# Down projection of a decoder trunk on one core: seven and eight pairs of K-blocks as seven products, instead of six and six

## The chip, the cores and the metric

The kernel runs on one core of a Trainium2 chip. The core has a matmul engine (TensorE; its weight loads are shown as a row of their own, PEld), VectorE (DVE), ScalarE (ACT), GpSimd (POOL) and SyncE (SP), whose queue issues nearly all loads. The metric is the device time of one execution in microseconds (us), less is better.

## The reference, cut to what matters

One layer of a decoder: a token mixer, and then the feed-forward part that this document is about. With 256 tokens, a model width of 2048 and a hidden width of 5632, all in float32:

```python
    h = rms_norm(x, pre_ffn_g[l])
    f = (jax.nn.silu(h @ w_gate[l]) * (h @ w_up[l])) @ w_down[l]
    x = x + rms_norm(f, post_ffn_g[l])
```

The product with `w_down` (5632 x 2048) is the down projection.

## The kernel before, in words

**Splitting.** Every float32 operand is split into a high part (`hi`, a cast on ScalarE) and a low part (`lo`, the difference, on VectorE). A product of two blocks is three matmuls into one PSUM bank: high by high, low by high and high by low (`product`, lines 664 to 666). Weights come from memory in pieces of 512 KB (128 partitions x 1024 numbers, two K-blocks by 512 columns) into four load buffers (`raw`), and their parts go into pools of five buffers each (`hi`, `lo`).

**Halves.** The down projection (`down_columns`) makes 1024 of the 2048 output columns in one call, as two chunks of 512, and is called twice: the first and the second half. In each the 44 K-blocks of 128 are taken as 22 pairs. A pair has 2 K-blocks, 2 token blocks of 128 and 2 chunks of columns, which is 8 products of blocks.

**Plain and seven-product pairs.** A plain pair (`plain_pair`, "P") does the 8 products, 24 matmuls. The other kind (`seven_products`, "S") gets the same 8 from 7 products of sums, as Strassen's scheme does, 21 matmuls. For that it needs sums of the hidden activations (`token_sums`, once for all columns) and sums of the weights (lines 629 and 635, on VectorE, in each half anew). The sums are split again: `hi_sb`/`lo_sb` and `hi_sa`/`lo_sa`. A P has two low parts to make, an S has a low part of 1024 columns, one of 512 (`lo_22`), four sums of 512 columns and two more low parts. TensorE takes the products of an S in the order of the tiles `hi`, `hi_22`, `hi_sb`, `hi_sa`; its 12th matmul is the first that reads `lo_sb`.

**Order.** A text of 20 letters gives the order of P and S pairs in a half; two plain pairs (20 and 21) close it, ordered by bank, so that the banks are done one after the other and can be closed: the partial sums of the S products are added (`partial_sums`, after the last S), squares are summed for the norm and gains multiplied (`close_chunk`, `close_last`), and at the very end the scaled output is stored (`scale_out`). In both halves the text is PPSPPSPPSPPSPPSPPSPP, with S for pairs 4 to 9. I count the steps of a half from 0. The engines run their queues in order; a framework places the instructions of each queue, somewhat ahead of the program's order.

Of the kernel before, what the change touches and what calls it, by code (L numbers as in the profile page):

```python
# [8 lines left out]
F32 = mybir.dt.float32  # L9
F32R = mybir.dt.float32r  # L10
AF = mybir.ActivationFunctionType
# [3 lines left out]
P = 128  # L15
# [18 lines left out]
def trunk(  # L34
# [23 lines left out]
    nc = tc.nc  # L58
# [70 lines left out]
    def load_in_order(dst, src):  # L129
        tc.keep_in_program_order(nc.sync.dma_start(out=dst, in_=src))  # L130
# [424 lines left out]
    hpool = ctx.enter_context(tc.tile_pool(name="hpool", bufs=1, side="right"))  # L555
# [4 lines left out]
    def h_chunk(c):  # L560

        if c not in h_parts:
            n = 2 if c < 8 else 1
            part = hpool.tile([P, 2, 4 * n, T], F32R, tag=f"h{c}", name=f"h{c}")
            for j in range(n):
                h_parts[c + j] = (part, 4 * j)
        part, k0 = h_parts[c]
        return part[:, 0, k0:k0 + 4], part[:, 1, k0:k0 + 4]
# [6 lines left out]
    sums = {}  # L575
# [189 lines left out]
    dn = ctx.enter_context(tc.tile_pool(name="dn", bufs=1))  # L765
    ss_f = const.tile([P, NT, 4], F32, tag="ss_f", name="ss_f")
# [3 lines left out]
    def hidden_sums(c):  # L770
        hi, lo = h_chunk(c)
        tmp = dn.tile([P, 2, 1024], F32, tag="wide", name="sums_f")
        home = dn.tile([P, 2, 2, 4, P], F32R, tag=f"sums{c}", name=f"sums{c}")
        token_sums(c, 2, hi, lo, tmp, home)

    def down_columns(n0, new_fg, seq, extra, finish, tail_pairs, order):

        gp = [ft.tile([P, 512], F32, tag="fa", name="gp") for _ in range(2)]
        for j in range(2):
            load_in_order(gp[j], post_ffn[(n0 + j) * 512:(n0 + j + 1) * 512].partition_broadcast(P))  # L780
        kinds = [k for k, _ in seq]
        last_s = max(i for i, k in enumerate(kinds) if k == "S")
        banks, product = products_into(kinds + ["P"] * len(tail_pairs), bank_in(dict(enumerate(
            ("tr", "acc", "acc", "acc", "tr", "mx", "mx", "acc")))))
        srcs = (w_down[n0], w_down[n0 + 1])
        for i, (k, p) in enumerate(seq):
            if i in extra:
                extra[i]()
            if k == "P":
                parts = plain_pair(srcs, p, h_of)  # L790
            else:
                h22 = dn.tile([P, 512], F32R, tag="h22", name="hi_22")
                l22 = dn.tile([P, 512], F32R, tag="l22", name="lo_22")
                parts = seven_products(srcs, p, h_of, sums[p // 2, p % 2], h22, l22)
            for part in parts:
                for b, a, w in part:
                    product(b, a, w)
            advance()
            if i == last_s:
                fg = new_fg()  # L800
                partial_sums(banks, fg[:, 0, 0:512], fg[:, 0, 512:1024], fg[:, 1, 0:512], fg[:, 1, 512:1024])
        parts = [plain_pair(srcs, p, h_of) for p in tail_pairs]
        where = {1: (0, 0), 2: (0, 1), 3: (1, 0), 7: (1, 1)}

        def run(*bs):
            for j in range(2):
                for prods in parts:
                    for b, a, w in prods[j]:
                        if b in bs:
                            product(b, a, w)  # L810

        for bs in order:
            run(*bs)
            for b in bs:
                finish(n0, *where[b], fg, banks[b], gp)

    def close_chunk(n0, tb, j, fg, bank, gp):
        cs = slice(j * 512, (j + 1) * 512)
        n = n0 + j
        nc.vector.tensor_tensor(out=fg[:, tb, cs], in0=fg[:, tb, cs], in1=bank, op=ALU.add)  # L820
        sq = dn.tile([P, 512], F32, tag="u", name="sq_f")
        nc.scalar.activation(out=sq, in_=fg[:, tb, cs], func=AF.Square, accum_out=ss_f[:, tb, n:n + 1])
        nc.vector.tensor_tensor(out=fg[:, tb, cs], in0=fg[:, tb, cs], in1=gp[j], op=ALU.mult)

    def sequence(pattern, s_pairs, p_pairs):
        s_it, p_it = iter(s_pairs), iter(p_pairs)
        return [(k, next(s_it if k == "S" else p_it)) for k in pattern]
# [3 lines left out]
    def new_fg(pool, tag):  # L831
        fgs.append(pool.tile([P, NT, 1024], F32, tag=tag, name=f"fg{len(fgs)}"))
        return fgs[-1]

    pattern = "PPSPPSPPSPPSPPSPPSPP"
    down_columns(0, lambda: new_fg(dn, "wide"), sequence(pattern, range(4, 10), [0, 1, 2, 3] + list(range(10, 20))),
                 {0: lambda: hidden_sums(2), 5: lambda: hidden_sums(3), 11: lambda: hidden_sums(4)}, close_chunk, [20, 21],
                 [(1, 3), (2, 7)])

    def scale_out(tb, chunks):  # L840
        for c in chunks:
# [6 lines left out]
    def close_last(n0, tb, j, fg, bank, gp):  # L848
        cs = slice(j * 512, (j + 1) * 512)
        n = n0 + j  # L850
        nc.vector.tensor_tensor(out=fg[:, tb, cs], in0=fg[:, tb, cs], in1=bank, op=ALU.add)
        sq = dn.tile([P, 512], F32, tag="u", name="sq_f")
        nc.scalar.activation(out=sq, in_=fg[:, tb, cs], func=AF.Square, accum_out=ss_f[:, tb, n:n + 1])
        if (tb, j) == (1, 0):
            scale_out(0, (1, 2))
        if j == 0:
            nc.vector.tensor_tensor(out=fg[:, tb, cs], in0=fg[:, tb, cs], in1=gp[j], op=ALU.mult)
            nc.vector.tensor_reduce(out=part_ss[:, tb:tb + 1], in_=ss_f[:, tb, 0:3], axis=AX.X, op=ALU.add)
            nc.vector.tensor_scalar(out=part_ss[:, tb:tb + 1], in0=part_ss[:, tb:tb + 1], scalar1=1.0 / D, scalar2=EPS,
                                    op0=ALU.mult, op1=ALU.add)  # L860
            return
        nc.vector.scalar_tensor_tensor(out=ss_t[:, tb:tb + 1], in0=ss_f[:, tb, 3:4], scalar=1.0 / D,
                                       in1=part_ss[:, tb:tb + 1], op0=ALU.mult, op1=ALU.add)
        nc.gpsimd.tensor_tensor(out=ro_f[:, tb:tb + 1], in0=ss_t[:, tb:tb + 1], in1=neg_half[:, :1], op=ALU.pow)
        nc.vector.tensor_tensor(out=fg[:, tb, cs], in0=fg[:, tb, cs], in1=gp[j], op=ALU.mult)
        if tb == 0:
            scale_out(0, (0,))
        else:
            scale_out(1, (0, 1, 2))
            scale_out(0, (3,))  # L870
            scale_out(1, (3,))

    down_columns(2, lambda: new_fg(hpool, "h0"), sequence(pattern, range(4, 10), [0, 1, 2, 3] + list(range(10, 20))),
                 {}, close_last, [20, 21], [(1,), (2,), (3,), (7,)])


def _layout(inputs):
# [86 lines left out]
```

## Time and profile before

| | us |
|---|---|
| median of 3 runs (1127.82 to 1128.39) | 1127.92 |
| the profiled execution's own time | 1127.93 |
| its span, first to last instruction | 1126.2 |
| TensorE busy in the span | 1113.6 |
| VectorE busy | 817.0 |
| ScalarE busy | 578.4 |

The profile is of one execution. Times of rows are us from the start of the span. The rest of the execution's own time, 1.7 us, lies around the span. An engine that is busy for a part of the span can still set the time of the stage in which others wait for it.

### The profile page before, as it was taken

To read this page: it belongs to the slowest core of one execution; us is meant where nothing else is said; L and a number is where in the kernel's file an instruction comes from. 1 tells how busy PE (TensorE), PEld (TensorE's weight loads), DVE (VectorE), ACT (ScalarE), POOL (GpSimd) and SP (SyncE) were. 2 spreads that over 40 slices of the span, in tenths; PEclk is the share of its full clock that TensorE was granted. 3 is DMA by queue.
4 is the path that set the end of the run, shared out by engine and by line. 5 is a ranking of instruction groups with operands and counts; after the bars stand their busy time and mean duration, and the time that the engine had idled before them with its cause. 6 is when DMAs were issued, how large, how long until landed. Compare 5 with 4: busy or idle time off the path is not lost.

```text
span 1126.2 us, 14203 instructions
## 1 busy us (share of the span) xinstructions
PE 1113.6 (99%) x5198; PEld 937.4 (83%) x5198; DVE 817.0 (73%) x1039; ACT 578.4 (51%) x792; POOL 27.5 (2%) x55
## 2 busy tenths in 40 slices
PE   9999999999999999999999999999999999999996
PEld 7888899998888878888888888888888888888885
DVE  6655555656778488797888987888655787777775
ACT  7644445655644356455455545445444454554451
POOL 0000000000200001000000000000000000000000
PEclk9999999999999999999999999999999999999998
DMA  9855555566566547467457457556655456665662
GB/s 355 267 190 185 169 161 182 162 217 194 170 195 235 186 148 227 154 195 235 164 183 239 157 187 233 178 187 221 204 192 187 145 191 225 220 214 194 213 213 86
DMA packets 65014, 221.35 MB, mean 197 GB/s; under 512 B 7344, under 2 KB 9392, under 8 KB 64432
## 3 DMA queue, kind: packets, MB, share of 16 engines
q1 hardware_dynamic: 64656, 220.30, 59.8%
q8 instruction: 40, 0.66, 0.2%
q14 instruction: 30, 0.25, 0.1%
q10 hardware_dynamic: 288, 0.15, 0.1%
HBM read 218.32 MB, written 2.10 MB: 196 GB/s over the span
## 4 chain that ended last, share of the span: by engine, by line
PE 96%; DVE 2%; DMA 1%; issue 1%; ACT 0%; POOL 0%; POOLq 0%; DVEq 0%; ACTq 0%; SPq 0%
PE bank L666 16%; PE bank L664 16%; PE bank L665 16%; PE acc L88 15%; PE acc L90 14%; PE acc L89 14%; PE h_ps L687 1%; DMA raw<-in_w_down_dram 1%; PE qk_ps L235 0%; PE sc L267 0%; DMA cols<-in_cols_dram 0%; PE yt_ps L191 0%; DVE x_lo L499 0%; DVE lo L81 0%; PE o_ps L243 0%
## 5 line engine op out<-in xcount | busy, mean ns | idle before, releaser
L81 DVE TENSOR_TENSOR lo<-raw,hi 128x1024 fp32r<-128x1024 f32 (+2 forms) x353 | 415.8, 1184 | 233.8 <-ACT hi L79 224.2
L79 ACT CAST hi<-raw 128x1024 fp32r<-128x1024 f32 (+2 forms) x353 | 358.0, 1018 | 341.4 <-PE acc L89 148.4
L88 PE MATMUL acc<-hi,x_hi 128*128 128x512 f32 (+1 forms) x640 | 244.5, 382 | 0.7 <-ACT x_hi L183 0.7
L89 PE MATMUL acc<-hi,x_lo 128*128 128x512 f32 (+1 forms) x640 | 239.5, 374 | 0.0
L90 PE MATMUL acc<-lo,x_hi 128*128 128x512 f32 (+1 forms) x640 | 239.2, 375 | 0.0
L664 PE MATMUL bank<-hi,x_hi 128*128 128x512 f32 x416 | 162.5, 391 | 0.0
L666 PE MATMUL bank<-lo,x_hi 128*128 128x512 f32 x416 | 161.9, 389 | 0.0
L665 PE MATMUL bank<-hi,x_lo 128*128 128x512 f32 x416 | 161.8, 389 | 0.0
L88 PEld LDWEIGHTS acc<-hi,x_hi 128*128 128x128 f32 x640 | 120.6, 188 | 19.5 <-issue 2.0
L90 PEld LDWEIGHTS acc<-lo,x_hi 128*128 128x128 f32 x640 | 120.5, 188 | 18.3
L89 PEld LDWEIGHTS acc<-hi,x_lo 128*128 128x128 f32 x640 | 120.7, 189 | 17.0 <-DVE x_lo L184 0.2
L664 PE MATMUL bank<-hi,h 128*128 128x512 f32 x280 | 109.1, 390 | 0.0
L665 PE MATMUL bank<-hi,h 128*128 128x512 f32 x280 | 108.9, 389 | 0.0
L666 PE MATMUL bank<-lo,h 128*128 128x512 f32 x280 | 108.9, 389 | 0.0
L666 PEld LDWEIGHTS bank<-lo,x_hi 128*128 128x128 f32 x416 | 78.1, 188 | 16.3
L665 PEld LDWEIGHTS bank<-hi,x_lo 128*128 128x128 f32 x416 | 78.1, 188 | 16.0
L664 PEld LDWEIGHTS bank<-hi,x_hi 128*128 128x128 f32 x416 | 78.1, 188 | 15.9
L634 ACT CAST hi_sb<-raw 128x1024 fp32r<-128x1024 f32 x28 | 29.4, 1051 | 112.7 <-DVE raw L629 103.3
L664 PEld LDWEIGHTS bank<-hi,h 128*128 128x128 f32 x280 | 52.6, 188 | 11.1 <-DVE h L691 0.4
L666 PEld LDWEIGHTS bank<-lo,h 128*128 128x128 f32 x280 | 52.6, 188 | 10.9
L665 PEld LDWEIGHTS bank<-hi,h 128*128 128x128 f32 x280 | 52.6, 188 | 10.9
L629 DVE TENSOR_TENSOR raw<-raw 128x512 f32<-128x512 f32 x84 | 58.0, 690 | 1.9
(214 smaller groups left out, 1210.0 us busy)
## 6 DMA issues: line engine op xcount, KB each, us to landing
raw<-in_w_gate_dram SPq DMA_DIRECT2D x88, 512.0 KB, 4.3
raw<-in_w_up_dram SPq DMA_DIRECT2D x88, 512.0 KB, 4.5
raw<-in_w_down_dram SPq DMA_DIRECT2D x88, 512.0 KB, 4.4
raw<-in_w_ret_dram SPq DMA_DIRECT2D x47, 512.0 KB, 4.2
raw<-in_w_diff_dram SPq DMA_DIRECT2D x48, 384.0 KB, 3.2
raw<-in_w_out_dram SPq DMA_DIRECT2D x32, 512.0 KB, 3.6
raw<-in_w_sgu_dram SPq DMA_DIRECT2D x16, 512.0 KB, 3.9
x_sb<-in_x_dram SPq DMA_DIRECT2D x2, 1024.0 KB, 8.3
```

Source lines behind the costliest of these rows:

```text
L79: nc.scalar.copy(out=hi, in_=raw)
L81: nc.vector.tensor_tensor(out=lo, in0=raw, in1=hi.bitcast(F32), op=ALU.subtract)
L88: nc.tensor.matmul(ps, lhsT=a_hi, rhs=wh, start=first, stop=False)
L89: nc.tensor.matmul(ps, lhsT=a_lo, rhs=wh, start=False, stop=False)
L90: nc.tensor.matmul(ps, lhsT=a_hi, rhs=wl, start=False, stop=last)
L629: nc.vector.tensor_tensor(out=out, in0=in0, in1=in1, op=op)
L634: nc.scalar.copy(out=h3, in_=rb)
L664: nc.tensor.matmul(banks[b], lhsT=a_hi, rhs=w_hi, start=start, stop=False)
L665: nc.tensor.matmul(banks[b], lhsT=a_lo, rhs=w_hi, start=False, stop=False)
L666: nc.tensor.matmul(banks[b], lhsT=a_hi, rhs=w_lo, start=False, stop=left[b] == 0)
L687: nc.tensor.transpose(out=pt[:, i], in_=aa[tb][:, i * P:(i + 1) * P], identity=ident)
```

## The change

The second letter text is replaced by two: the first half gets a seventh S (pair 10), the second half a seventh and an eighth (pairs 10 and 11). Pairs 10 and 11 need token sums of their own (`sums_10`, `sums_11`), made one pair at a time. Their tiles take space that is free by then; for that the hidden chunks 0 and 1, which shared a tile, get one each. The squares of the closing steps, whose values nobody reads (only their sum), are written into the PSUM bank that was just read instead of a buffer of their own.

```diff
-            n = 2 if c < 8 else 1
+            n = 2 if 2 <= c < 8 else 1
...
+    def hidden_sums_of_pair(c, q, tmp, home):
+        hi, lo = h_chunk(c)
+        token_sums((c, q), 1, hi[:, 2 * q:2 * q + 2], lo[:, 2 * q:2 * q + 2], tmp, home)
+        sums[c, q] = sums[(c, q), 0]
+
+    def sums_10():
+        hidden_sums_of_pair(5, 0, dn.tile([P, 2, 512], F32, tag="wide", name="sums_f"),
+                            dn.tile([P, 2, 1, 4, P], F32R, tag="sums5", name="sums5"))
+
+    def sums_11():
+        hidden_sums_of_pair(5, 1, hpool.tile([P, 2, 512], F32, tag="h0", name="sums_f"),
+                            hpool.tile([P, 2, 1, 4, P], F32R, tag="h1", name="sums11"))
...
-        sq = dn.tile([P, 512], F32, tag="u", name="sq_f")
-        nc.scalar.activation(out=sq, in_=fg[:, tb, cs], func=AF.Square, accum_out=ss_f[:, tb, n:n + 1])
+        nc.scalar.activation(out=bank, in_=fg[:, tb, cs], func=AF.Square, accum_out=ss_f[:, tb, n:n + 1])
...
-    pattern = "PPSPPSPPSPPSPPSPPSPP"
-    down_columns(0, lambda: new_fg(dn, "wide"), sequence(pattern, range(4, 10), [0, 1, 2, 3] + list(range(10, 20))),
-                 {0: lambda: hidden_sums(2), 5: lambda: hidden_sums(3), 11: lambda: hidden_sums(4)}, close_chunk, [20, 21],
-                 [(1, 3), (2, 7)])
+    down_columns(0, lambda: new_fg(dn, "wide"),
+                 sequence("PPSPPSPPSPPSPSPSPSPP", range(4, 11), [0, 1, 2, 3] + list(range(11, 20))),
+                 {0: lambda: hidden_sums(2), 5: lambda: hidden_sums(3), 9: lambda: hidden_sums(4), 13: sums_10},
+                 close_chunk, [20, 21], [(1, 3), (2, 7)])
...
-    down_columns(2, lambda: new_fg(hpool, "h0"), sequence(pattern, range(4, 10), [0, 1, 2, 3] + list(range(10, 20))),
-                 {}, close_last, [20, 21], [(1,), (2,), (3,), (7,)])
+    down_columns(2, lambda: new_fg(hpool, "h0"),
+                 sequence("PPSPPSPSPSPPSPSPSPSP", range(4, 12), [0, 1, 2, 3] + list(range(12, 20))),
+                 {9: sums_11}, close_last, [20, 21], [(1,), (2,), (3,), (7,)])
```

How the queues change, at three places. First SyncE's queue in the second part of the first half (lines with - stood there before, lines with + stand there now). L77 loads the pieces of plain pairs, L601 those of S pairs; "x4" are four equal ones in a row.

```order
 L77 DMA raw<-in_w_down_dram 128x1024 x4
 L601 DMA raw<-in_w_down_dram 128x1024 x2
-L77 DMA raw<-in_w_down_dram 128x1024 x4
-L601 DMA raw<-in_w_down_dram 128x1024 x2
-L77 DMA raw<-in_w_down_dram 128x1024 x4
+L77 DMA raw<-in_w_down_dram 128x1024 x2
+L601 DMA raw<-in_w_down_dram 128x1024 x2
+L77 DMA raw<-in_w_down_dram 128x1024 x2
+L601 DMA raw<-in_w_down_dram 128x1024 x2
+L77 DMA raw<-in_w_down_dram 128x1024 x2
 L601 DMA raw<-in_w_down_dram 128x1024 x2
 L77 DMA raw<-in_w_down_dram 128x1024 x12
```

From step 11 on two loads of a plain pair, and no longer four, stand between those of two S pairs.

Second, VectorE's queue at step 8 of the first half, an S pair (`lo`, `lo_22`, here with its number, the sums of weights, `lo_sb`, `lo_sa`), as it was before:

```order
L605 TENSOR_TENSOR lo<-raw,hi 128x1024
L605 TENSOR_TENSOR lo_7893<-raw,hi_7892 128x512
L629 TENSOR_TENSOR raw<-raw 128x512 x3
L635 TENSOR_TENSOR raw<-raw 128x512
L605 TENSOR_TENSOR lo_sb<-raw,hi_sb 128x1024
L605 TENSOR_TENSOR lo_sa<-raw,hi_sa 128x1024
```

and as it is now, from `lo_22` on, with the token sums of pair 10 (`sums_f`) between:

```order
L605 TENSOR_TENSOR lo_7894<-raw,hi_7893 128x512
L629 TENSOR_TENSOR raw<-raw 128x512
L582 TENSOR_TENSOR sums_f<-h_5606 128x512
L629 TENSOR_TENSOR raw<-raw 128x512
L586 SCALAR_TENSOR_TENSOR sums_f<-sums_f 128x128
L629 TENSOR_TENSOR raw<-raw 128x512
L587 SCALAR_TENSOR_TENSOR sums_f<-sums_f 128x128
L635 TENSOR_TENSOR raw<-raw 128x512
L589 TENSOR_TENSOR sums_f<-sums_f 128x128
L590 TENSOR_TENSOR sums_f<-sums_f 128x128
L605 TENSOR_TENSOR lo_sb<-raw,hi_sb 128x1024
L605 TENSOR_TENSOR lo_sa<-raw,hi_sa 128x1024
```

Five operations have come into this S pair, ahead of `lo_sb`. (The sums of chunk 4, too, stand where they stood, at step 5.)

Third, the end of the second half on VectorE, from the last S on: low parts of plain pairs (L81), the adding of partial sums (L673 to L676) and the first closing operation (L851 before, L863 now). Before:

```order
L605 TENSOR_TENSOR lo_sa<-raw,hi_sa 128x1024
L81 TENSOR_TENSOR lo<-raw,hi 128x1024 x3
L673 TENSOR_TENSOR fg_9177<-fg_9177,bank_8581 128x512
L674 TENSOR_TENSOR fg_9177<-fg_9177,bank_8585 128x512
L81 TENSOR_TENSOR lo<-raw,hi 128x1024
L675 TENSOR_TENSOR fg_9177<-fg_9177,bank_8577 128x512
L676 TENSOR_TENSOR fg_9177<-fg_9177,bank_8577 128x512
L81 TENSOR_TENSOR lo<-raw,hi 128x1024 x4
L851 TENSOR_TENSOR fg_9177<-fg_9177,bank_8479 128x512
```

and now:

```order
L605 TENSOR_TENSOR lo_sa<-raw,hi_sa 128x1024
L81 TENSOR_TENSOR lo<-raw,hi 128x1024 x3
L673 TENSOR_TENSOR fg_9255<-fg_9255,bank_8596 128x512
L81 TENSOR_TENSOR lo<-raw,hi 128x1024
L674 TENSOR_TENSOR fg_9255<-fg_9255,bank_8600 128x512
L81 TENSOR_TENSOR lo<-raw,hi 128x1024
L675 TENSOR_TENSOR fg_9255<-fg_9255,bank_8592 128x512
L676 TENSOR_TENSOR fg_9255<-fg_9255,bank_8592 128x512
L81 TENSOR_TENSOR lo<-raw,hi 128x1024
L863 TENSOR_TENSOR fg_9255<-fg_9255,bank_8494 128x512
```

The last S has moved one step nearer to the end: six low parts stand behind it and no longer eight, and the four additions stand right ahead of the last of them.

## Rows read from the trace of the kernel before

**Rows 1.** The page, part 4: the chain that ended last, by engine.

```profile
PE 96%; DVE 2%; DMA 1%; issue 1%; ACT 0%; POOL 0%; POOLq 0%; DVEq 0%; ACTq 0%; SPq 0%
```

**Rows 2.** Busy us (instructions) of PE, PEld, DVE, ACT, POOL; clock, DMA share, GB/s.

```profile
950.00:1000.00 50.00, 50.00 (x222) 41.42 (x221) 38.85 (x41) 26.74 (x31) 0.00 (x0) 1.00 0.69 229
```

**Rows 3.** Waits of TensorE's weight loads, 895 to 1127: us, times, longest.

```profile
PEld bank L666 <- DVE lo_sb L605: 0.5, 1, 0.5
```

**Rows 4.** Order in time, ScalarE: start, us, operation, [idle before, its releaser].

```profile
1099.78 1.05 ACT L79 CAST hi<-raw 128x1024 fp32r<-128x1024 f32 x1 [1.67 <-PE bank L665]
1102.50 1.05 ACT L79 CAST hi<-raw 128x1024 fp32r<-128x1024 f32 x1 [1.67 <-PE bank L665]
```

**Rows 5.** Order in time, ScalarE: the cast of an S pair's second block.

```profile
1065.26 0.62 ACT L624 CAST hi<-raw 128x512 fp32r<-128x512 f32 x1 [1.15 <-DMA raw<-in_w_down_dram]
```

**Rows 6.** Order in time, VectorE: the same S pair from `lo_22` on.

```profile
1065.92 0.69 DVE L605 TENSOR_TENSOR lo<-raw,hi 128x512 fp32r<-128x512 f32 x1 [0.54 <-ACT hi L624]
1066.53 2.14 DVE L629 TENSOR_TENSOR raw<-raw 128x512 f32<-128x512 f32 x3
...
1069.86 1.23 DVE L605 TENSOR_TENSOR lo_sb<-raw,hi_sb 128x1024 fp32r<-128x1024 f32 x1 [0.47 <-ACT hi_sb L634]
1071.00 1.22 DVE L605 TENSOR_TENSOR lo_sa<-raw,hi_sa 128x1024 fp32r<-128x1024 f32 x1
```

**Rows 7.** Order in time, SyncE's queue: the load issued behind that `lo_sa`.

```profile
1072.25 0.33 SPq L77 DMA_DIRECT2D raw<-in_w_down_dram  x1
```

**Rows 8.** Loads issued at 930.06, 944.85, 959.73, 974.61, 1056.17 (second ones), 1055.04 (a first).

```profile
raw<-in_w_down_dram SPq DMA_DIRECT2D x1, 512.0 KB, 4.8
raw<-in_w_down_dram SPq DMA_DIRECT2D x1, 512.0 KB, 4.6
raw<-in_w_down_dram SPq DMA_DIRECT2D x1, 512.0 KB, 4.2
raw<-in_w_down_dram SPq DMA_DIRECT2D x1, 512.0 KB, 6.0
raw<-in_w_down_dram SPq DMA_DIRECT2D x1, 512.0 KB, 4.1
raw<-in_w_down_dram SPq DMA_DIRECT2D x1, 512.0 KB, 3.4
```

**Rows 9.** Order in time, VectorE, first half: S pairs of steps 8, 11 and 14.

```profile
927.67 1.23 DVE L605 TENSOR_TENSOR lo_sb<-raw,hi_sb 128x1024 fp32r<-128x1024 f32 x1 [0.47 <-ACT hi_sb L634]
...
942.46 1.22 DVE L605 TENSOR_TENSOR lo_sb<-raw,hi_sb 128x1024 fp32r<-128x1024 f32 x1 [0.47 <-ACT hi_sb L634]
943.60 1.22 DVE L605 TENSOR_TENSOR lo_sa<-raw,hi_sa 128x1024 fp32r<-128x1024 f32 x1
...
958.48 1.22 DVE L605 TENSOR_TENSOR lo_sa<-raw,hi_sa 128x1024 fp32r<-128x1024 f32 x1
```

**Rows 10.** Order in time, TensorE: the first use of `lo_sb`, steps 8, 11; second half's step 5.

```profile
929.58 0.39 PE L666 MATMUL bank<-lo_sb,sums 128*128 128x512 f32 x1
...
945.22 0.39 PE L666 MATMUL bank<-lo_sb,sums 128*128 128x512 f32 x1
...
1029.54 0.39 PE L666 MATMUL bank<-lo_sb,sums 128*128 128x512 f32 x1
```

**Rows 11.** Order in time, VectorE, gate and up projection: token sums of one pair.

```profile
440.01 0.29 DVE L590 TENSOR_TENSOR sums_f<-sums_f 128x128 f32<-128x128 f32 x1
440.23 1.23 DVE L81 TENSOR_TENSOR lo<-raw,hi 128x1024 fp32r<-128x1024 f32 x1
```

**Rows 12.** Order in time, VectorE: `lo_sa` of the second half's step 5.

```profile
1023.68 1.22 DVE L605 TENSOR_TENSOR lo_sa<-raw,hi_sa 128x1024 fp32r<-128x1024 f32 x1
```

**Rows 13.** Order in time, VectorE: the first and the second closing operation.

```profile
1108.17 0.69 DVE L851 TENSOR_TENSOR fg<-fg,bank 128x512 f32<-128x512 f32 x1 [3.36 <-PE bank L666]
...
1110.89 0.69 DVE L851 TENSOR_TENSOR fg<-fg,bank 128x512 f32<-128x512 f32 x1 [0.29 <-PE bank L666]
```

**Rows 14.** Order in time, ScalarE: the last square of the first half, and its accumulator.

```profile
1002.21 0.63 ACT L822 ACTIVATE sq_f<-fg 128x512 f32<-128x512 f32 x1
1002.75 0.19 ACT L822 ACTIVATION_READ_ACCUMULATOR sq_f<-fg 128x1 f32 x1
```

More of the change, by code (lines that the diff above doesn't have):

```diff
@@ L851, in close_last @@
         nc.vector.tensor_tensor(out=fg[:, tb, cs], in0=fg[:, tb, cs], in1=bank, op=ALU.add)
-        sq = dn.tile([P, 512], F32, tag="u", name="sq_f")
-        nc.scalar.activation(out=sq, in_=fg[:, tb, cs], func=AF.Square, accum_out=ss_f[:, tb, n:n + 1])
+        nc.scalar.activation(out=bank, in_=fg[:, tb, cs], func=AF.Square, accum_out=ss_f[:, tb, n:n + 1])
         if (tb, j) == (1, 0):
```

## The prediction

> **What bounds the kernel now.** I read the page first, then the chain that ended last, the busy times by stage, the waits of TensorE, and last the order in time of the queues that feed it. TensorE holds 96% of the chain [rows 1]. In the down projection (1020 matmuls, 231 us at the price below) TensorE has no gap, while VectorE is busy 38.85 of the 50 us shown, or 78% [rows 2]. The one wait for weights in the first half's early steps is 0.5 us, for `lo_sb`, the low part of the third set of weights of a seven-product pair [rows 3]; so that tile is the one to watch, and what follows counts how early it is.
>
> The price of a matmul: ScalarE's casts near the end are each released when TensorE has done 12 matmuls with a tile, and they come 2.72 us apart, so one matmul is 2.72 / 12 = 0.2267 us [rows 4]. A plain pair (P, 24 matmuls) is 5.44 us, a seven-product pair (S, 21) is 4.76 us.
>
> **What the change takes away.** One more S in the first half and two more in the second: 3 x 3 = 9 matmuls, 9 x 0.2267 = 2.04 us. That is the whole gain, and it's less than the 0.2% (2.26 us) that a measurement of this kernel can tell from no change. So the sum is about what the new order costs.
>
> **What an S pair needs.** One can be followed in the order in time of ScalarE and VectorE. Its second weight block lands, ScalarE casts `hi_22` at 1065.26, VectorE makes `lo_22` at 1065.92, four sums from 1066.53, waits for ScalarE's `hi_sb`, makes `lo_sb` (1069.86, ends 1071.09) and `lo_sa` (1071.00, ends 1072.22) [rows 5, 6]. From landing to the end of `lo_sb` that is 0.02 + 5.83 us, to the end of `lo_sa` 0.02 + 6.96 us. There are four load buffers and every pair takes two. An S holds its two until `lo_sb` and `lo_sa` are written, and SyncE issues the next loads into them 0.03 us later [rows 7].
>
> In PPS the S's loads go into buffers of the plain pair two steps before, which are free long before. In PSPS they go into those of the S before. So each S waits for the S before it, once round this loop: 0.03 us to issue, the load, 0.02 us, 6.96 us. The eleven loads of the down projection that were issued 1.14 us behind another, as these will be, took 4.1 to 6.0 us with a median of 4.5 [rows 8]. The loop is then 0.03 + 4.5 + 0.02 + 6.96 = 11.51 us, and TensorE needs 45 x 0.2267 = 10.20 us for S and P. Each turn loses 1.31 us of whatever VectorE is ahead; after that, TensorE waits 1.31 us per turn. No row of before shows PSPS; the loop is put together from these rows.
>
> A page speaks to the load. The Trainium skill (DMA: Bandwidth & Descriptors, section on the anatomy of one DMA) fits 2.0 us plus bytes over 436 GB/s to loads that GpSimd issues, which is an estimate of 3.2 us for 512 KB. By that figure the loop would take about 10.6 us, the waits all but vanish, and the time would come out near 1126.2 us. The rows differ, and they decide: on SyncE's queue the quickest load shown took 3.4 us, the quickest second one 4.1 us [rows 8].
>
> **First half.** How far ahead is VectorE when the alternation begins at step 11 (steps counted from 0)? In before `lo_sb` of step 8 ends at 927.67 + 1.23 = 928.90 [rows 9] and TensorE first uses it at 929.58 [rows 10]: 0.68 in hand. The order puts the new token sums of pair 10 into that S: one operation of 512 columns (0.61 us from start to start, as `lo_22` in [rows 6]) and four of 128 columns (440.01 to 440.23: 0.22 us each [rows 11]). That is 1.49 us, but the sums of weights wait for each other (0.72 apart, not 0.60) and `lo_sb` waits 0.47 us for its cast [rows 6], which hides part: counted through, `lo_sb` is 0.55 us later, 0.13 in hand, no wait. The delay stays to step 11, as the loads in between are issued when these tiles are done. There `lo_sb` ends at 942.46 + 1.23 + 0.55 = 944.24, used at 945.22, and `lo_sa` at 943.60 + 1.22 + 0.55 = 945.37 [rows 9, 10].
>
> Step 13: `lo_sb` ends at 945.37 + 0.03 + 4.5 + 0.02 + 5.83 = 955.75; TensorE wants it at 945.22 + 10.20 = 955.42. Late by 0.33. Steps 15 and 17 add 1.31 each: 2.95 us of waits, less one S's 0.68, is +2.27 us. Behind step 17 stand four plain pairs before the next S, and the lag is made up.
>
> **Between the halves.** The squares now go into the PSUM banks, so the second half's first matmuls wait for ScalarE and not for VectorE. The last square starts at 1002.21 and with its accumulator is done at 1002.94 [rows 14]. The second half starts at 1029.54 - 128 x 0.2267 = 1000.52, and needs that bank 15 matmuls later, at 1003.92. So it costs nothing, with 1.0 us to spare; without that cover it would cost the excess once.
>
> **Second half**, in the times of before. `lo_sa` of step 5 ends at 1023.68 + 1.22 = 1024.90 [rows 12], `lo_sb` is used at 1029.54 [rows 10]. In step 6 the second low part needs a tile that TensorE holds to the start of step 5 (1029.54 - 11 x 0.2267 = 1027.05); behind it come the last sums operation, the cast of step 7 (its tile is free six matmuls later), `lo`, `lo_22` and the 5.69 us from the sums of weights to the end of `lo_sa`: 1037.07. Step 9: 1037.07 + 11.51 = 1048.58, `lo_sb` 2.49 us in hand. Two plain pairs follow, for which I take the spacing of before, 958.48 - 943.60 = 14.88 us [rows 9], against 15.64 us on TensorE: 3.25 in hand at step 12. Steps 14, 16, 18: 1.94, 0.63, and 0.68 late. The waits are 0.68 us, the two S save 1.36 us.
>
> **The end.** `lo_sa` of step 18 ends at 1097.99. In before VectorE had done all weights 3.4 us ahead of the first closing operation, at 1108.17 [rows 13]. Now six low parts (1.14 us each from start to start) and the four operations that add up the partial sums (0.60 each) stand between, and the loads for the last pairs come late. In the new queue's order they end at 1099.1 and 1100.2 (step 19), 1102.5 (pair 20: load issued at 1096.89, 3.4 us, cast 1.05), 1103.1, 1104.7 (load issued at 1098.02, 4.5 us, cast), 1105.3, 1106.5, 1107.1, 1107.7, 1108.8. So the first closing operation starts at 1108.82, and the next, 2.72 - 0.29 = 2.43 us behind it by [rows 13], at 1111.25 in place of 1110.89: the end is 0.36 us later, although TensorE is done 0.68 us sooner. **Sum:** +2.27 + 0.36 = +2.63 us on the profiled execution's 1127.93 us (its span is 1126.21), which is the median of the three runs to 0.01 us: **1130.6 us**.
>
> Both ends of the load's time: with 4.2 us [rows 8] the first half costs 2.05 - 0.68 = +1.37, the second waits for nothing and ends 1.14 us sooner: +0.2, 1128.2 us. With 4.8 us [rows 8]: 3.85 - 0.68 = +3.17 and +1.86: +5.0, 1132.9 us. So 0.1 us of load time is worth 0.8 us, since every loop of both halves adds up.
>
> **Rivals.**
> 1. Loads at the quick end, so no change that can be measured: the same loops at 4.1 to 4.45 us, 1127.4 to 1130.2 us. For it: 4.1 and 4.2 [rows 8]. Against: the alternation issues four loads 1.14 us apart, and where the first half did that the second took 4.2 to 6.0. It decides from 4.45 us down.
> 2. A load as slow as 6.0 us [rows 8] inside an alternating stretch: 1.5 us more than 4.5, each time it meets one with nothing in hand, 1132.1 us for one. One in eleven was so slow, and about six loops count.
> 3. The gain comes through: loads of 3.4 us (the first of a group [rows 8]) make the loop 10.8 us, 0.8 us of waits in the first half, none in the second: -1.2 us, 1126.7 us. No second load was that quick. It's the way the Trainium skill's figure would lead.
> 4. VectorE is further ahead at step 11 than I count (the sums hidden wholly): 0.55 us less, 1130.0 us; inside the range.
>
> **How the numbers follow.** Forecast (loads 4.45 to 4.8 us) 0.42, rival 2 0.14, rival 1 with 4 0.34, rival 3 0.10. Slower by over 0.2% (above 1130.2): 0.42 + 0.14 less a little for a late load that falls where there is slack, 0.54. Faster needs more than the 2.04 us of matmuls: 0.03. Same 0.43. The range takes the quick loads to 1127.5 and one slow load upon 4.6 us to 1133.2; rival 3 and two slow loads are left out.
>
> **What will show it.** Right: TensorE waits for `lo_sb` at steps 13, 15 and 17 of the first half, about 0.3, 1.3 and 1.3 us, and at step 18 of the second; ScalarE's `hi_22` there released by the load; loads issued just behind `lo_sb` and `lo_sa`; more time between the last load and the first closing operation. TensorE's busy time 2 us shorter and its waits longer. Wrong: no waits at steps 13 to 17 (the loop is shorter than 10.2 us, or VectorE further ahead), waits at step 8 or for `hi` tiles, or a late start of the second half (the banks).

## The result and the profile after

The changed kernel takes 1134.34 us (median of 5 runs, 1132.76 to 1138.48); the kernel before, on the same chip, 1128.09 (5 runs, 1127.82 to 1128.39). The ratio is 1.0060, with the 95% interval [1.0048, 1.0071]: slower, as forecast, but by 6.2 us where 2.6 were foreseen, and 1.1 us above the upper end of the range. The profiled run is the median run, with a span of 1132.62 us, 6.41 more than before's 1126.21. One run among all those below took 1396.05 us, with a granted clock of 0.752 where the others have 0.989 to 0.998; it is left out.

The page's part 4 of the kernel after, the chain by engine (before: [rows 1]):

```profile
PE 92%; DVE 3%; DMA 2%; issue 1%; ACT 1%; POOLq 0%; POOL 0%; DVEq 0%; ACTq 0%
```

TensorE's share of the chain fell from 96% to 92%; VectorE, ScalarE and the loads have a point more each. The busy times by stretch, columns as in [rows 2], kernel after:

```profile
950.00:1000.00 50.00, 48.83 (x211) 38.84 (x210) 40.75 (x45) 26.86 (x31) 0.00 (x0) 1.00 0.64 218
...
1050.00:1100.00 50.00, 49.23 (x214) 39.50 (x212) 38.09 (x42) 22.73 (x25) 0.00 (x0) 1.00 0.56 190
```

In the first of these stretches TensorE did 211 matmuls, where before did 222 [rows 2]. VectorE is busy 38 of 50 us in the second, no more than in before's stretches, so it waits too. What TensorE's weight loads waited for, kernel after, first half from 895 us on (us, times, longest):

```profile
PEld bank L666 <- DVE lo_sb L605: 3.3, 5, 1.0
PEld bank L664 <- ACT hi_sb L634: 0.8, 2, 0.5
PEld bank L664 <- DVE h L691: 0.4, 1, 0.4
```

and second half:

```profile
PEld bank L666 <- DVE lo_sb L605: 2.3, 3, 1.0
PEld bank L664 <- ACT hi_sb L634: 2.2, 2, 1.7
PEld bank L666 <- DVE lo L81: 0.9, 1, 0.9
PEld bank L664 <- ACT bank L834: 0.2, 1, 0.2
```

Before had one wait of 0.5 us for `lo_sb` in the whole stretch [rows 3]. Now there are eight, and `hi_sb`, made just ahead of it, is late too. (The wait of 0.4 us for `h`, early in the down projection, is in before as well.) The chain of waits at step 16 of the second half, kernel after (start, us, what), shows the whole loop once:

```profile
1078.23 1.23 DVE lo_sa L605
...
1079.47 4.40 DMA raw<-in_w_down_dram
...
1083.97 0.63 ACT hi L624
...
1084.62 0.69 DVE lo L605
1085.31 0.61 DVE raw L629
...
1085.95 0.70 DVE raw L629
...
1086.67 0.70 DVE raw L629
...
1087.47 1.06 ACT hi_sb L634
...
1088.55 1.24 DVE lo_sb L605
...
1089.83 0.51 PE bank L666
```

It starts with `lo_sa` of the S at step 14: that frees the second load buffer, the load starts right behind it, takes 4.40 us, and then cast, low part, three sums, cast and low part follow each other with 0.1 us or less between. TensorE is at the end of it. The two `lo_sa` in VectorE's order in time:

```profile
1078.23 1.22 DVE L605 TENSOR_TENSOR lo_sa<-raw,hi_sa 128x1024 fp32r<-128x1024 f32 x1
...
1089.69 1.22 DVE L605 TENSOR_TENSOR lo_sa<-raw,hi_sa 128x1024 fp32r<-128x1024 f32 x1
```

They end at 1079.44 and 1090.91 (rounded rows); that is 11.47 us, where the prediction put 11.51.

The span, split by three rows of TensorE's order in time (first matmul of each half, last matmul), kernel after:

```profile
883.60 0.39 PE L664 MATMUL bank<-hi,h 128*128 128x512 f32 x1
...
1002.90 0.39 PE L664 MATMUL bank<-hi,h 128*128 128x512 f32 x1
...
1121.60 0.39 PE L666 MATMUL bank<-lo,h 128*128 128x512 f32 x1
```

and before:

```profile
883.42 0.39 PE L664 MATMUL bank<-hi,h 128*128 128x512 f32 x1
...
1000.53 0.39 PE L664 MATMUL bank<-hi,h 128*128 128x512 f32 x1
...
1115.90 0.39 PE L666 MATMUL bank<-lo,h 128*128 128x512 f32 x1
```

So:

| us | predicted | measured |
|---|---|---|
| up to the down projection | 0 | +0.18 |
| first half (117.11 to 119.30) | +2.27 | +2.19 |
| second half, to its last matmul (115.37 to 118.70) | -0.68 | +3.33 |
| from the last matmul to the end (10.31 to 11.02) | +1.04 | +0.71 |
| span | +2.63 | +6.41 |

Nearly all of the miss of this profile lies in the second half: 4.69 us of waits there, and not 0.68. (A wait here is the time from one matmul's start to the next beyond 0.2267 us; before's second half has none.)

### The profile page after: what moved, and what is told of

Same layout as the page of the kernel before. It is cut to its first block, busy times and chain, and to the rows that moved or that the text cites. A ratio compares the mean times of both kernels' runs of the same rounds, so it can differ in the third digit from the quotient of the medians.

```text
span 1132.6 us, 14233 instructions
## 1 busy us (share of the span) xinstructions
PE 1115.3 (98%) x5189; PEld 935.1 (83%) x5189; DVE 832.7 (74%) x1069; ACT 582.2 (51%) x800; POOL 27.6 (2%) x55
## 4 chain that ended last, share of the span: by engine, by line
PE 92%; DVE 3%; DMA 2%; issue 1%; ACT 1%; POOLq 0%; POOL 0%; DVEq 0%; ACTq 0%
PE bank L666 15%; PE bank L664 15%; PE bank L665 15%; PE acc L88 15%; PE acc L90 15%; PE acc L89 15%; DMA raw<-in_w_down_dram 2%; DVE raw L629 1%; PE h_ps L687 1%; DVE lo_sb L605 1%; PE qk_ps L235 0%; PE sc L267 0%; DVE lo L605 0%; ACT hi_sb L634 0%; DVE lo L81 0%
## 5 line engine op out<-in xcount | busy, mean ns | idle before, releaser
L81 DVE TENSOR_TENSOR lo<-raw,hi 128x1024 fp32r<-128x1024 f32 (+2 forms) x347 | 408.1, 1184 | 212.8 <-ACT hi L79 204.3
L79 ACT CAST hi<-raw 128x1024 fp32r<-128x1024 f32 (+2 forms) x347 | 350.7, 1016 | 316.7 <-PE acc L89 147.0
L666 PE MATMUL bank<-lo,h 128*128 128x512 f32 x262 | 102.1, 390 | 0.5 <-DVE lo L81 0.5
L664 PE MATMUL bank<-hi,h 128*128 128x512 f32 x262 | 102.2, 390 | 0.0
L665 PE MATMUL bank<-hi,h 128*128 128x512 f32 x262 | 102.0, 389 | 0.0
L634 ACT CAST hi_sb<-raw 128x1024 fp32r<-128x1024 f32 x31 | 32.5, 1049 | 121.7 <-DVE raw L629 108.9
L629 DVE TENSOR_TENSOR raw<-raw 128x512 f32<-128x512 f32 x93 | 64.2, 690 | 2.0
L605 DVE TENSOR_TENSOR lo<-raw,hi 128x1024 fp32r<-128x1024 f32 (+1 forms) x46 | 48.0, 1050 | 19.7 <-ACT hi L623 16.2
L666 PEld LDWEIGHTS bank<-lo,h 128*128 128x128 f32 x262 | 49.2, 188 | 11.0 <-DVE lo L81 0.9
L664 PEld LDWEIGHTS bank<-hi,h 128*128 128x128 f32 x262 | 49.2, 188 | 10.7 <-DVE h L691 0.4
```

What stands on the lines that cost most here:

```text
L79: nc.scalar.copy(out=hi, in_=raw)
L81: nc.vector.tensor_tensor(out=lo, in0=raw, in1=hi.bitcast(F32), op=ALU.subtract)
L605: nc.vector.tensor_tensor(out=lo, in0=raw, in1=hi.bitcast(F32), op=ALU.subtract)
L629: nc.vector.tensor_tensor(out=out, in0=in0, in1=in1, op=op)
L634: nc.scalar.copy(out=h3, in_=rb)
L664: nc.tensor.matmul(banks[b], lhsT=a_hi, rhs=w_hi, start=start, stop=False)
```

## The experiments

"Same chip" medians of before are given with each. Edits are against the changed kernel unless another is named.

**One half each, and neither.** The first run has the second half of before, the second one the first half of before (the sums of pair 10 are still made), the third both:

```diff
-                 sequence("PPSPPSPSPSPPSPSPSPSP", range(4, 12), [0, 1, 2, 3] + list(range(12, 20))),
-                 {9: sums_11}, close_last, [20, 21], [(1,), (2,), (3,), (7,)])
+                 sequence("PPSPPSPPSPPSPPSPPSPP", range(4, 10), [0, 1, 2, 3] + list(range(10, 20))),
+                 {}, close_last, [20, 21], [(1,), (2,), (3,), (7,)])
```

> The first half as in the change (a seventh S pair, alternating), the second half as before with six. Theory (an S pair's loads wait for the buffers of the S before, a loop of some 11.5 us against 10.2 us on TensorE): the waits of steps 13 to 17, 2.5 us in the profile of the change, less 0.68 us of matmuls: +1.8 to +2.3 us on before, 1129.9 to 1130.4. Rival (the first half's lag costs more later, in the second half too): above 1131.

> The second half as in the change (eight S pairs, alternating), the first half's order as before with six; the token sums of pair 10 are still made there, as the second half needs them. The profile of the change has some 4.5 us of waits in the second half and an end 0.7 us later. Theory (part of it is the lag that the first half hands on, 0.8 us less in hand at step 5): +2.3 to +3.2 us, 1130.4 to 1131.3. Rival (the second half alone does it, its own loads being slow): +3.8 us or more, 1131.9 and up.

> Both halves in the order of before with six S pairs; only the squares go into the PSUM banks, and the hidden chunks 0 and 1 have tiles of their own. Theory (these edits cost nothing, the banks are free 1.0 us before they are needed): 1127.7 to 1128.4, as before. Rival (the banks hold up the start of the second half, or the last closing): slower by 0.3 us or more.

Before's median was 1128.45 for all three. First half alone: 1132.15 us, ratio 1.0035 [1.0023, 1.0048]: +3.70. Second half alone: 1130.88, 1.0024 [1.0014, 1.0033]: +2.43. The small edits (squares into the banks, the tiles of `h`): 1127.92, 0.9996 [0.9987, 1.0005]: nothing. 3.70 + 2.43 = 6.13, and the whole change is 6.25 over its own before. So the halves add up, as far as intervals of 1.4 and 1.1 us to either side tell. The second run lies in the range expected for a lag that the first half hands on, but such a lag doesn't show: with the first half of before, the second still waits 4.28 us in its profile (of a run 1.1 us above the median), against 4.69 in the changed kernel. The first run lies where its rival was put, above 1131, but not for the rival's reason: its second half waits 0.5 us in all. Its first half cost more than expected; the second loads of the S pairs at steps 13, 15 and 17 took 4.89, 5.01 and 4.84 us there (4.36, 4.25, 4.23 in the changed kernel's profile), and its waits beyond before's were 4.64 us, not 2.87.

**S pairs with load buffers of their own** (all fifteen S). The buffers lie in the residual's tile, so these two kernels leave the residual out of the last addition. The second run, with the order of before and its twelve S, is the control. Of the edit, the part that loads:

```diff
-        ra, rb = (fetch(src[p]) for src in srcs)
+        if own_raw:
+            k = 2 * (own_raw[1] % 2)
+            own_raw[1] += 1
+            ra, rb = own_raw[0][:, k], own_raw[0][:, k + 1]
+            for raw, src in zip((ra, rb), srcs):
+                nc.sync.dma_start(out=raw, in_=src[p])
+        else:
+            ra, rb = (fetch(src[p]) for src in srcs)
```

> The whole change, but the S pairs of the down projection load into four buffers of their own, in the place of the residual x (the last addition adds the scaled product itself and not x, so the residual is left out; the number and shape of operations stay). So an S pair waits for the buffers of the S two before it. Theory (load buffers): the waits at steps 13 to 18 vanish, and the matmuls' 2.04 us come through, less up to 0.6 us at the end: 1126.0 to 1126.8. Rival (VectorE's own work of 9.9 us for an S and a P, with its waits for casts, is the bound, or the five weight tiles are): waits of 2 us and more stay, 1129 to 1133.

> The control of the run with own load buffers: the order of before (6 and 6), S pairs loading into four buffers of their own; the residual is left out there too. Theory: the order of before waits 1.5 us in all, 0.4 of it for an S pair, so own buffers are worth 0.5 us at most: 1127.4 to 1128.2 us, and the order of after with own buffers (1126.18) stays 1.2 to 2.0 us below it, as 9 matmuls are 2.04 us. Rival (own buffers make any order faster, so the run with them says nothing on the alternation): 1126.6 us or less.

With the changed order 1126.18 us (before 1128.45; 0.9980 [0.9971, 0.9989]); with the order of before 1127.77 (before 1128.52; 0.9994 [0.9985, 1.0002]). The busy times of the changed order with own buffers:

```profile
950.00:1000.00 50.00, 50.00 (x222) 41.40 (x221) 41.63 (x45) 27.08 (x32) 0.00 (x0) 1.00 0.69 223
1050.00:1100.00 50.00, 50.00 (x223) 41.39 (x222) 43.12 (x48) 26.13 (x29) 0.00 (x0) 1.00 0.50 166
```

TensorE has no gap, while VectorE is busy 43.12 of 50 us, five more than in the changed kernel. VectorE had the time; what it lacked was the data in time. The sums of pair 11 stand at step 9 here, as in the change. The 9 matmuls are worth 1126.18 - 1127.77 = -1.6 us between these two (2.04 by their price).

**The same number of S pairs, spread out.** First half S at steps 2, 5, 8, 11, 14, 17, 19, second half at 0, 2, 5, 8, 10, 13, 15, 17:

```diff
-                 sequence("PPSPPSPPSPPSPSPSPSPP", range(4, 11), [0, 1, 2, 3] + list(range(11, 20))),
+                 sequence("PPSPPSPPSPPSPPSPPSPS", range(4, 11), [0, 1, 2, 3] + list(range(11, 20))),
-                 sequence("PPSPPSPSPSPPSPSPSPSP", range(4, 12), [0, 1, 2, 3] + list(range(12, 20))),
+                 sequence("SPSPPSPPSPSPPSPSPSPP", range(4, 12), [0, 1, 2, 3] + list(range(12, 20))),
```

> The same fifteen seven-product pairs (7 and 8), but fewer of them directly behind one plain pair: S at steps 2, 5, 8, 11, 14, 17, 19 of the first half and 0, 2, 5, 8, 10, 13, 15, 17 of the second. Theory (load buffers): only an S two steps behind an S loses lead, 1.3 to 1.6 us, and an S three steps behind one gains about 0.7; one turn in the first half with over 1 us in hand and four in the second with over 4 us in hand and three gains between them: no TensorE wait over 0.5 us, the 9 matmuls (2.04 us) come through, 1125.9 to 1127.0 us. Rival (fifteen S pairs are too much work for VectorE or the loads wherever they stand): 1130 us or more.

1135.38 us (before 1128.52; 1.0066 [1.0054, 1.0078]): a clear miss. The first half was nearly as hoped (2.30 us of waits in all, 0.6 of it at step 8; before 1.51). The S at step 0 of the second half was not; the waits of TensorE's weight loads, 1000 to 1010:

```profile
PEld bank L664 <- ACT hi_sb L634: 1.6, 1, 1.6
PEld bank L666 <- DVE lo_sb L605: 1.0, 1, 1.0
PEld bank L666 <- DVE lo_sa L605: 0.7, 1, 0.7
PEld bank L666 <- DVE lo L81: 0.3, 1, 0.3
```

Its sums of weights share VectorE with the closing operations of the first half, and the lead (how early `lo_sb` is done before TensorE uses it) was gone before the tight turns began: step 0 alone waits 3.8 of the half's 8.2 us. Behind it the lead at steps 5 and 8, each three behind an S, was 0.2 us, and step 13, three behind one too, waited, as did steps 10, 15 and 17: PPS didn't bring the lead back, with second loads of 5.4 to 6.4 us at steps 5, 8 and 13. The theory's "an S three steps behind one gains about 0.7" is too kind; the 4.2 us that the changed kernel has at step 2 come with the plain pairs around the start of the half.

**The second load on another queue.**

```diff
-        ra, rb = (fetch(src[p]) for src in srcs)
+        ra, rb = (wraw.tile([P, 2, 512], F32, tag="raw", name="raw") for _ in srcs)
+        nc.sync.dma_start(out=ra, in_=srcs[0][p])
+        (nc.gpsimd if act_of is h_of else nc.sync).dma_start(out=rb, in_=srcs[1][p])
```

> The changed kernel, with the second load of each S pair of the down projection issued by GpSimd, not SyncE; buffers and order as in the change. It tells apart why the second load takes 4.2 to 5.2 us where the first takes 3.4. Theory A (it waits behind the first on the same queue): on a queue of its own it lands in about 3.4 us, the loop falls to about 10.4 us against TensorE's 10.2, nearly all waits in the alternation go, 1127 to 1129.5 us. Theory B (both share the DMA engines, whatever the queue): still 4.2 us or more, 1132 to 1137 us as the changed kernel.

1141.2 us (6 runs, 1136.72 to 1148.82; before 1128.52; 1.0128 [1.0098, 1.0157]). Three of GpSimd's loads, issued at 945.79, 957.23 and 1080.27:

```profile
raw<-in_w_down_dram POOLq DMA_DIRECT2D x1, 512.0 KB, 4.1
...
raw<-in_w_down_dram POOLq DMA_DIRECT2D x1, 512.0 KB, 4.3
...
raw<-in_w_down_dram POOLq DMA_DIRECT2D x1, 512.0 KB, 8.4
```

Of nine (steps 13, 15, 17 of the first half, 7, 9, 12, 14, 16, 18 of the second) eight took 3.9 to 5.2 us, and the one of step 16 8.4. So another queue doesn't make the second load as quick as theory A has it, about 3.4: theory B, though the time is above its range of 1132 to 1137 us. In the profile, of a run of 1138.32 us, step 16 alone waits 6.5 us, and GpSimd issues these loads 0.3 us behind `lo_sa`, where SyncE takes 0.03. The Trainium skill (DMA: Bandwidth & Descriptors, section on the anatomy of one DMA on the GpSimd path) fits loads so issued to 2.0 us plus bytes over 436 GB/s, which gives an estimate of 3.2 us for 512 KB. None of the nine, each with another load under way, was as quick; the measurement decides.

**The last S of the second half a plain pair.**

```diff
-                 sequence("PPSPPSPSPSPPSPSPSPSP", range(4, 12), [0, 1, 2, 3] + list(range(12, 20))),
-                 {9: sums_11}, close_last, [20, 21], [(1,), (2,), (3,), (7,)])
+                 sequence("PPSPPSPSPSPPSPSPSPPP", range(4, 11), [0, 1, 2, 3] + list(range(11, 20))),
+                 {}, close_last, [20, 21], [(1,), (2,), (3,), (7,)])
```

> The changed kernel with the last S of the second half (step 18) a plain pair, 7 and 7 seven-product pairs in all. By the prediction's price the wait there was 0.68 us, which is the gain of one S: no difference to the changed kernel's 1134.3 us (within 0.5). By the trace of the changed kernel step 18 is 2.3 us late and pair 20 waits 0.7 us more behind it, for 0.68 us of matmuls: 1131.0 to 1132.8 us. If the waits only move on to pair 20 and the closing operations: above 1133.5 us.

1131.09 us (before 1128.52; 1.0030 [1.0018, 1.0042]), 2.57 over its before where the whole change is 6.25 over: that one S costs 3.7 us, and it was put at nothing. The time is in the range worked out from the changed kernel's trace. Waits of weight loads in its second half:

```profile
PEld bank L664 <- ACT hi_sb L634: 1.2, 1, 1.2
PEld bank L666 <- DVE lo_sb L605: 1.0, 1, 1.0
```

Both belong to step 16, for which the second load took 5.9 us. Steps 18 and pair 20 don't wait.

**The ring broken, the whole computation.** The ring is that of the four load buffers, in which, where P and S alternate, each S waits for the S before it. Two idle tiles of 8 KB a partition serve as load buffers for the S at step 15 of the first half and at steps 9, 14 and 18 of the second; the sums of pair 11 move to step 7 (the run with own buffers had no waits with them at step 9, so the move isn't what takes them away). In the second run the first half is that of before:

```diff
+    def room_in(pool, tag):
+        return lambda: pool.tile([P, 2, 2, 512], F32, tag=tag, name="own_raw")
+
+    apart = {(2, i): room_in(hpool, "h0") for i in (9, 14, 18)}
+    apart[0, 15] = room_in(dn, "wide")
...
+            if (n0, i) in apart:
+                room = apart[n0, i]()
+                own.append((room[:, 0], room[:, 1]))
...
+        if own:
+            ra, rb = own.pop()
+            nc.sync.dma_start(out=ra, in_=srcs[0][p])
+            nc.sync.dma_start(out=rb, in_=srcs[1][p])
```

> The whole computation with the changed order of pairs. S pairs at step 15 of the first half and at steps 9, 14 and 18 of the second load into two buffers of their own, in 8 KB a partition that are idle then (the tile of the token sums' work, and that of the first activations), so that no S but those at step 13 and step 7 waits for the S two steps before it; the sums of pair 11 are made at step 7, not 9. Theory (the loop through the load buffers): at most 1 us of waits at step 13, none behind it, none in the second half; the 2.04 us of matmuls come through: 1126.2 to 1127.4 us, below both kernels. Rival A (slow loads, wherever they go) and rival B (VectorE has no time for S pairs this close): the waits at steps 14, 16 and 18 of the second half stay, 1130 us or more.

> As the run with the ring broken, with the first half of the kernel before (six S pairs) and the sums of pair 10 at its step 13. Theory: no waits in the second half, its two more S pairs are worth 1.36 us against before's 1128.4: 1126.7 to 1127.6 us, 3.3 to 4.2 us under the same order in the ring (1130.88). Rivals A and B as there: 1129.5 us or more.

Broken in both halves: 1127.9 us (ten runs of 1126.06 to 1128.77; before 1128.31; 0.9996 [0.9987, 1.0005]). Against its before it is 6.6 us better than the change, but 0.5 above the expected range: steps 5, 8 and 13 of the first half wait, 2.3 us by the weight loads; the loads for step 8 and the second one of the plain pair before it took 6.1 to 6.4 us. In the second half there is no wait at all, with the same eight S pairs at the same steps.

Broken in the second half alone: 1126.83 us (before 1128.31; 0.9987 [0.9978, 0.9996]), below before and the change, and 4.1 us under the same order in the ring (1130.88), within the 3.3 to 4.2 expected. The busy times of its second half:

```profile
1050.00:1100.00 50.00, 50.00 (x222) 41.41 (x221) 42.81 (x47) 27.25 (x30) 0.00 (x0) 1.00 0.58 201
```

The changed kernel shows 49.23 and 38.09 for TensorE and VectorE in this stretch. The loads into the added buffers were not quicker (second ones 4.9 to 7.0 us). They were issued earlier, and landed in time.

**A seventh S at the end of the first half**, against the run above:

```diff
-                 sequence("PPSPPSPPSPPSPPSPPSPP", range(4, 10), [0, 1, 2, 3] + list(range(10, 20))),
-                 {0: lambda: hidden_sums(2), 5: lambda: hidden_sums(3), 11: lambda: hidden_sums(4), 13: sums_10},
+                 sequence("PPSPPSPPSPPSPPSPPSPS", range(4, 11), [0, 1, 2, 3] + list(range(11, 20))),
+                 {0: lambda: hidden_sums(2), 5: lambda: hidden_sums(3), 9: lambda: hidden_sums(4), 13: sums_10},
```

> As the run with the ring broken in the second half alone (1126.83), but the first half has its seventh S pair at step 19, behind a plain pair, where in the spread order 0.9 us were in hand, and no other alternation. Theory: no wait at step 19, four plain pairs follow before the second half's first S, so the lead is made up there; 0.68 us of matmuls more than that run: 1125.9 to 1126.8 us. Rival (the lead lost at step 19 comes back as a wait at step 2 or 5 of the second half, as step 0 did in the spread order): 1127 us or more.

1131.08 us (6 runs, 1128.67 to 1134.52; before 1128.17; 1.0032 [1.0020, 1.0044]): the rival, though at another place than it said. Step 19 doesn't wait; the second half's first pair does, 2.2 us. VectorE there (start, us, operation):

```profile
1001.49 1.21 DVE L81 TENSOR_TENSOR lo<-raw,hi 128x1024 fp32r<-128x1024 f32 x1
1002.63 0.68 DVE L605 TENSOR_TENSOR lo<-raw,hi 128x512 fp32r<-128x512 f32 x1
1003.23 1.27 DVE L848 TENSOR_TENSOR fg<-fg,bank 128x512 f32<-128x512 f32 x2
```

and TensorE:

```profile
1004.71 0.50 PE L671 MATMUL bank<-hi,h 128*128 128x512 f32 x1 [2.06 <-ACT bank L849]
```

The profile is of the quickest of the six runs, so what makes the others up to 5.9 us longer isn't seen. The closing sums of the first half (L848) stand in VectorE's queue behind low parts of the next pairs. When those come late, ScalarE squares the bank late, and TensorE waits for the bank.

## Why the prediction was wrong, step by step

**The step that failed is the second half's "The waits are 0.68 us".** They were 4.69 us. The lead, that is the time from the end of `lo_sb` on VectorE to its first use on TensorE, worked out from these two rows at each S (below zero: the wait there). The rows of steps 9 and 12, kernel after, VectorE:

```profile
1049.46 1.23 DVE L605 TENSOR_TENSOR lo_sb<-raw,hi_sb 128x1024 fp32r<-128x1024 f32 x1 [0.47 <-ACT hi_sb L634]
...
1065.07 1.23 DVE L605 TENSOR_TENSOR lo_sb<-raw,hi_sb 128x1024 fp32r<-128x1024 f32 x1 [0.47 <-ACT hi_sb L634]
```

and TensorE:

```profile
1052.43 0.39 PE L666 MATMUL bank<-lo_sb,sums 128*128 128x512 f32 x1
...
1068.07 0.39 PE L666 MATMUL bank<-lo_sb,sums 128*128 128x512 f32 x1
```

All seven steps, us:

| step of the second half | 5 | 7 | 9 | 12 | 14 | 16 | 18 |
|---|---|---|---|---|---|---|---|
| predicted | | | 2.49 | 3.25 | 1.94 | 0.63 | -0.68 |
| changed kernel | 5.00 | 3.11 | 1.74 | 1.77 | -0.20 | -1.22 | -2.33 |
| second half alone | 5.16 | 3.56 | 2.03 | 2.64 | 1.06 | -0.85 | -1.34 |

Where the prediction lets a lead go on falling past zero, the table shows a new wait at each step, since a wait resets the lead. Four things add up in the changed kernel:

1. *The lead at step 9 was 1.74, not 2.49.* It was 5.00 at step 5, where before's rows gave 5.78 (1023.76 to 1029.54). The lack is there at step 2 already (4.21, before 5.22), and from step 5 to 9 the lead falls by 3.26, as forecast (3.29). Ahead of step 2 VectorE waits for the cast of that S pair's second block, which before it doesn't, kernel after:

```profile
1003.47 0.69 DVE L605 TENSOR_TENSOR lo<-raw,hi 128x512 fp32r<-128x512 f32 x1 [0.72 <-ACT hi L624]
```

The block's load took 4.68 us and landed at 1002.80. That wait is 0.88 and 1.34 us in the runs of the first and the second half alone, both with 4.22 in hand at step 2, and 0.19 with the last S plain, which has 4.93 there and 5.72 at step 5, with the same first half as the change.

2. *PPS gave back 0.03 us, not 0.76*, from step 9 to 12. I took the spacing from before, where the lead is so large that nothing waits for a load in PPS [rows 9]. Here the two plain pairs and the S behind them get their buffers close together, and six loads are issued within 8 us (1050.71 to 1058.71), kernel after:

```profile
raw<-in_w_down_dram SPq DMA_DIRECT2D x6, 512.0 KB, 5.6
```

Their median is 5.6 us, against the 4.5 of the sum. The runs of the second half alone and with the last S plain, where the same six loads have medians of 5.1 and 4.8, got 0.61 and 0.63 back.

3. *The turns to steps 14, 16 and 18 cost 5.5 us together (1.77 in hand, and 3.75 of waits), not 3 x 1.31 = 3.93.* The second loads took 4.64, 4.40 and 5.20, against 4.5. Two more waits joined the loop. At step 14 ScalarE's `hi_sb` waited for TensorE to give back a tile of high parts, kernel after:

```profile
1076.00 1.05 ACT L634 CAST hi_sb<-raw 128x1024 fp32r<-128x1024 f32 x1 [3.18 <-PE bank L666]
```

And at step 18 the first load took 5.05, so that `lo` of the first block held up `lo_22`. These two loops took 12.01 and 12.56 us, where the formula (0.03 + load + 0.02 + 6.96) gives 11.65 and 12.21. The other three loops of this half, to steps 7, 9 and 16, follow the formula: 12.08, 11.57 and 11.47 us with loads of 5.01, 4.49 and 4.40, for 12.02, 11.50 and 11.41. (Waits for `hi` tiles stood among the prediction's signs of being wrong.)

4. *Pair 20 waits 0.73 us (1.57 in the second half alone).* It loads into the buffers of the S at step 18, so it's the ring once more. I followed its tiles only for the closing operations, never for TensorE.

1.48 less lead at step 12 (points 1 and 2), 1.6, 0.7, and 0.2 in two small waits, at the bank of pair 0 and at the end, make 4.0.

**What held.** *The loop through the load buffers* is the cause: the chain above, 11.47 us where 11.51 was put together, and the ring-broken runs, which take all waits of the second half away with the same order, the same sums and as many loads. *First half:* 0.13 us in hand at step 8 (0.06, and a wait of 0.11), none at step 11 (1.05 in hand, forecast 0.98), waits of 0.36, 1.10 and 1.05 at steps 13, 15 and 17 (forecast 0.33, 1.31, 1.31). The sum, +2.19 for +2.27, is partly luck: loads there were 4.2 to 4.4 us against the 4.5 of the sum, the waits beyond before's were 2.87 us, and the two other profiles of this first half have 3.88 and 4.64. By the medians of the runs of one half each, the first half missed by 1.4 us (3.70 for 2.27) and the second by 2.1 (2.43 for 0.36). *Edits at nothing:* 0.9996. *Between the halves:* a wait of 0.07 us in the changed kernel, but 0.4 and 0.5 in the runs of one half each, and 2.2 with a late seventh S. So "it costs nothing, with 1.0 us to spare" holds only while low parts are early, since the closing sums queue behind them. *"The lag is made up":* nearly, 4.21 us in hand at the second half's step 2 where before has 5.22, and the halves add up.

**The end.** The last of the low parts and the first closing operation, kernel after, VectorE:

```profile
1113.69 1.22 DVE L81 TENSOR_TENSOR lo<-raw,hi 128x1024 fp32r<-128x1024 f32 x1
1114.82 0.69 DVE L863 TENSOR_TENSOR fg<-fg,bank 128x512 f32<-128x512 f32 x1
```

As foreseen VectorE has no time in hand here; before it idled 3.36 us [rows 13]. The operation starts 6.0 us later than the 1108.82 of the prediction, as TensorE is late too; what follows the last matmul grew by 0.71 us, against 1.04.

**The rivals.** The result lies above all four. Nearest is rival 2 (a slow load in an alternating stretch): it gave one such load 0.14, and 1132.1 us. In the changed kernel's profile the S at step 18 has one of 5.2 us, and those of the plain pair behind it 6.6 and 6.8. My sensitivity, 0.8 us for 0.1 us of load, doesn't explain the miss: the second loads of the eight turns (4.2 to 5.2 us) took 4.57 us in the mean, and 0.07 us above 4.5 is worth 0.6 us by it. What failed is the rest of the second half's sum: the lead and the give-back of PPS, taken from rows of an order in which TensorE hardly ever waits for a load, and the waits that it left out. Two readings were loose besides. Rival 3's loop of 10.8 us with loads of 3.4 (and the 10.6 beside 3.2) isn't the sum's own, which is 10.41 (10.21); where the 0.4 comes from isn't said. And the "eleven loads" are the second ones of groups; others issued 1.14 us behind another, mostly third or fourth in their group, took up to 6.3 us in before.

**A sign that didn't come.** TensorE's busy time was to be 2 us shorter; the page has 1115.3 us, before 1113.6. In the down projection the changed kernel waits 9.1 us (4.38 and 4.69), but only 4.2 us of it stand as gaps in TensorE's busy time: the page shows a matmul for 0.39 us and more, where the next can start after 0.23. The waits have to be read from the starts.

## What to carry to other kernels

When a change packs the users of a small ring of buffers closer, write down the loop release, load, use, release, and compare it with what the bound engine needs for the same steps; if it's longer, every turn pays, and the busy share of VectorE (78% here) doesn't show it. The Trainium skill (Perfetto Trace Analysis, section on identifying performance opportunities) says that the same gap repeating on an engine that should be saturated can mean too few buffers; here the repeated gap of 1.1 us went when two idle tiles became load buffers. Spacing the users out is no substitute where other work takes the lead, as the spread order showed, and leads, and what a stretch gives back, measured in a relaxed order are no price for a tight one.

## What the runs showed of the hardware

- In the changed kernel's turns a load of 512 KB mostly took 3.4 to 3.6 us as the first of a group (4.4 and 5.05 once each), 4.2 to 5.2 as the second, up to 6.8 as a later one. From GpSimd's queue the second one took 3.9 to 5.2 us, and once 8.4.
- The orders that wait for loads scatter more from run to run. The changed kernel's five runs lie 5.7 us apart and those with GpSimd's loads 12.1, while the run with own buffers, which doesn't wait for them, has eleven within 0.7 us. That the scatter of the loads makes the difference is likely, but no run shows it.
